# Merging the first input loads of a matmul kernel and giving one head cast to GpSimd

## The chip, the cores and the metric

One core of one Trainium2 chip. The metric is the device time of one execution in microseconds (us). TensorE is called PE in the profile, its weight load PEld, VectorE DVE, ScalarE ACT, GpSimd POOL, SyncE SP. All loads but the small one of the bias, and all stores, are issued by SP, and each of them is spread over 16 DMA engines. PSUM is the memory in which TensorE leaves its results; an eviction takes them out of it. A DMA has "landed" when the trace records its completion. The "head" is the part before the steady stream of tiles, some 18 us.

## The reference

```python
x = randn(16, 512, 1024); weight = randn(1024, 768)
bias = randn(768);        residual = randn(16, 512, 768)      # all float32
out = matmul(x, weight) + bias + residual
```

The kernel treats x as 8192 rows: 64 "tiles" of 128 rows, in 8 groups (S) of 8. Partition p of group S holds 8 consecutive rows; a load of "tiles 0 to 2" brings three rows of 1024 numbers to each of 128 partitions.

## The kernel before

Each tile is cast to bf16, transposed on TensorE (as four blocks of packed pairs), copied out of PSUM by VectorE, multiplied by the bf16 weights in 16 matmuls, evicted with bias or residual by VectorE, added to by GpSimd, and stored. In the head the first three tiles share the weights as they arrive. The parts that matter (cuts marked `...`):

```python
    load_x(0, 0, 2)
    load_x(0, 2, 3)
    load_w(0); load_w(1); load_w(2); load_w(3)
    load_x(0, 3, 4)
    load_x(0, 4, 6)
    load_x(0, 6, 8)
    load_res(0, 0, 4)
    load_x(1, 0, 4)
    ...
    keep_warm(12)                 # dummy matmuls, 128x512
    cast(0, "dve")
    cast(1)                       # ScalarE
    transp(0)                     # TensorE transposes into pt[t % 2], VectorE copies to xt
    transp(1)
    keep_warm(3)
    cast(2)
    transp(2)
    ...                           # bias broadcast by four matmuls, weight casts
    cast(HEAD, "dve")             # HEAD = 3: tile 3
    cast(HEAD + 1)
    for c in range(n_c):          # n_c = 4 blocks of the weights
        for t in range(HEAD):
            mms(t, 2 * c)
            mms(t, 2 * c + 1)
            if c == n_c - 1 and t == 0:
                finish(0)         # VectorE eviction
                pool_add(0)
            if c == n_c - 1 and t == 1:
                transp(HEAD)
    finish(1)
    ...
    for t in range(HEAD, n_t):    # steady state, one tile after another
        cast(t + 2)
        ...
```

## Time and profile before

| quantity | value | view |
|---|---|---|
| time | 210.83 us (210.65 to 210.95) | three runs |
| span of the profiled run | 209.0 us | page |
| TensorE busy | 200.4 us, 96% | page, part 1 |
| DMA queue q1 | 97.9% of 16 engines, 87.03 MB | page, part 3 |
| TensorE's last work ends | 203.06 us | chain of waits |
| last store issued, landed | 203.54 us, 205.19 to 208.13 us by engine | trace records |

From the page of the kernel before: busy times, then the DMA row of the 40 slices (tenths), the queue, and the chain by engine and by line.

```profile
PE 200.4 (96%) x1274; PEld 130.6 (63%) x1299; DVE 105.0 (50%) x139; ACT 67.6 (32%) x68; POOL 115.5 (55%) x71
...
DMA  6999999999999999999999999999999999999994
...
q1 hardware_dynamic: 5616, 87.03, 97.9%
...
PE 96%; issue 1%; DVE 1%
PE po L104 79%; PE pt L95 13%; PE po L170 3%; PE po L190 1%; DVE xt L99 0%; DVE ro L131 0%; DVE warm L156 0%
```

Two resources look full. To choose between them, follow the chain of waits in order of time (columns: start us, duration us, what). L170 are dummy matmuls, L95 transposes, L190 the bias matmuls, L104 the real matmuls.

```profile
1.19 5.26 PE po L170 x12
6.45 0.87 PE pt L95 x8
7.33 0.65 PE po L170 x3
7.97 0.44 PE pt L95 x4
8.41 1.29 PE po L190 x4
9.70 2.92 PE po L104 x18
...
199.15 3.91 PE po L104 x24
203.06 0.02 issue
203.08 0.42 DVE ro L131
```

It reads like a pure TensorE kernel, in which a late head would be paid at the end. But the chain stops at 203.50 us, the end of the last eviction, and the span is 209.0 us; the last 5.5 us, in which the last stores land, are in no share of the chain. The windows view covers them (first column: the stretch; last two: busy share of the 16 DMA engines, GB/s).

```profile
203.00:204.00 1.00, 0.05 (x1) 0.00 (x0) 0.42 (x1) 0.00 (x0) 0.00 (x0) 1.00 0.98 403
204.00:205.00 1.00, 0.00 (x0) 0.00 (x0) 0.00 (x0) 0.00 (x0) 0.00 (x0) 1.00 0.95 374
205.00:206.00 1.00, 0.00 (x0) 0.00 (x0) 0.00 (x0) 0.00 (x0) 0.00 (x0) 1.00 0.66 255
206.00:207.00 1.00, 0.00 (x0) 0.00 (x0) 0.00 (x0) 0.00 (x0) 0.00 (x0) 1.00 0.31 116
207.00:208.00 1.00, 0.00 (x0) 0.00 (x0) 0.00 (x0) 0.00 (x0) 0.00 (x0) 0.83 0.10 35
```

When TensorE ends, the DMA engines are still nearly full (0.98, then 0.95), and they then run dry one by one. The trace also records 16 landings for each of these DMAs, which I read as one from each engine. For the last store (128 KB, issued at 203.54) they are, in us, sorted:

```
205.19 205.22 205.25 205.38 205.52 205.56 206.38 206.43 206.56 206.65 206.69 206.83 206.84 207.32 208.06 208.13
```

The quickest engine lands its share 1.65 us after the issue. The slowest takes 4.59 us. My reading is that it still has older work in its queue; then the difference, 2.94 us, is roughly how much later the last store could be issued without moving the end.

The head of the kernel before, from the timeline (start us, duration us, engine, line, operation, count, [idle before, and what ended it]):

```profile
5.40 1.05 ACT L87 CAST xb<-x_tile 128x1024 bf16<-128x1024 f32 x1 [1.89 <-DMA x_tile<-in_x_dram]
5.40 0.69 DVE L87 CAST xb<-x_tile 128x1024 bf16<-128x1024 f32 x1 [4.13 <-DMA x_tile<-in_x_dram]
6.65 1.05 ACT L87 CAST xb<-x_tile 128x1024 bf16<-128x1024 f32 x1 [0.20 <-DMA x_tile<-in_x_dram]
...
15.47 0.70 DVE L87 CAST xb<-x_tile 128x1024 bf16<-128x1024 f32 x1 [0.71 <-DMA x_tile<-in_x_dram]
16.24 0.96 DVE L129 TENSOR_TENSOR tmp<-po,bias_sb 128x768 f32<-128x768 f32 x1
...
17.32 0.69 DVE L99 COPY xt<-pt 128x512 f32<-128x512 f32 x1
...
18.07 1.09 PEld L104 LDWEIGHTS <-xt 128*128 128x128 bf16 x8 [0.52 <-DVE xt L99]
```

The first two tiles are cast at 5.40 us, the third at 6.65 us, tile 3 at 15.47 us, and tile 3's matmuls, the start of the steady stream, begin at 18.07 us.

### The profile page before, as it was taken

The page shows a single profiled execution, that of the slowest core. Times are in us where ns is not written, and L with a number is a line of the kernel's source. Part 1 is how long each engine was busy: PE and PEld are TensorE (multiplying, and loading weights), DVE is VectorE, ACT ScalarE, POOL GpSimd, SP SyncE. Part 2 cuts the span into 40 slices and gives each one's busy share as a digit, 9 for nine tenths or more (in the row PEclk, how much of TensorE's full clock was granted, in tenths as well). Part 3 has the DMA queues.
Part 4 walks back from the last instruction along what each step waited for, and adds up shares of the span by engine and source line. Part 5 has one row for each costly group of instructions (what it writes and reads, how often), then busy time and mean ns, then how long its engine had stood idle before and what let it go on. Part 6 is the DMA issues. An engine that isn't in the chain of part 4 may idle for free.

```text
span 209.0 us, 3151 instructions
## 1 busy us (share of the span) xinstructions
PE 200.4 (96%) x1274; PEld 130.6 (63%) x1299; DVE 105.0 (50%) x139; ACT 67.6 (32%) x68; POOL 115.5 (55%) x71
## 2 busy tenths in 40 slices
PE   7999999999999999999999999999999999999980
PEld 2566666666666666666666666666666666666650
DVE  0737465445445544554554455455445544545550
ACT  2544315511723062422443054230724233430000
POOL 2000197819965565999189802994069910799000
PEclk9999999999999999999999999999999999999998
DMA  6999999999999999999999999999999999999994
GB/s 239 427 421 431 436 413 440 442 405 436 423 470 422 419 428 398 459 420 436 433 400 472 416 427 447 412 439 412 437 445 414 445 419 427 442 419 428 426 404 168
DMA packets 5632, 87.23 MB, mean 417 GB/s; under 512 B 625, under 2 KB 753, under 8 KB 1906
## 3 DMA queue, kind: packets, MB, share of 16 engines
q1 hardware_dynamic: 5616, 87.03, 97.9%
q8 instruction: 10, 0.16, 0.3%
q14 instruction: 4, 0.03, 0.0%
q10 hardware_dynamic: 2, 0.00, 0.0%
HBM read 61.87 MB, written 25.17 MB: 416 GB/s over the span
## 4 chain that ended last, share of the span: by engine, by line
PE 96%; issue 1%; DVE 1%
PE po L104 79%; PE pt L95 13%; PE po L170 3%; PE po L190 1%; DVE xt L99 0%; DVE ro L131 0%; DVE warm L156 0%
## 5 line engine op out<-in xcount | busy, mean ns | idle before, releaser
L104 PE MATMUL po<-w_sb,xt 128*128 128x512 bf16 (+1 forms) x999 | 175.4, 324 | 1.4
L104 PEld LDWEIGHTS <-xt 128*128 128x128 bf16 x1024 | 100.1, 98 | 59.5 <-DVE xt L99 0.5
L87 ACT CAST xb<-x_tile 128x1024 bf16<-128x1024 f32 x62 | 62.8, 1044 | 114.5 <-DMA x_tile<-in_x_dram 56.9
L121 POOL TENSOR_TENSOR ro<-ro,bias_sb 128x768 f32<-128x768 f32 x40 | 71.2, 1816 | 36.2 <-DMA ro<-in_residual_dram 26.2
L99 DVE COPY xt<-pt 128x512 f32<-128x512 f32 x64 | 44.2, 691 | 86.7 <-PE pt L95 86.5
L121 POOL TENSOR_TENSOR ro<-ro,tmp 128x768 f32<-128x768 f32 x24 | 43.1, 1814 | 41.0 <-DMA ro<-in_residual_dram 30.2
L131 DVE TENSOR_TENSOR ro<-po,ro 128x768 f32<-128x768 f32 (+2 forms) x41 | 38.0, 930 | 2.9 <-PE po L104 2.8
L95 PE MATMUL pt<-ident,xb 128*128 128x128 f32 x256 | 38.2, 273 | 0.0
L95 PEld LDWEIGHTS pt<-ident,xb 128*128 128x128 f32 x256 | 29.8, 141 | 8.1 <-issue 0.6
L129 DVE TENSOR_TENSOR tmp<-po,bias_sb 128x768 f32<-128x768 f32 x24 | 22.8, 949 | 0.6 <-POOL ro L121 0.5
L170 PE MATMUL po<-warm 128*128 128x512 bf16 x15 | 6.1, 579 | 1.2 <-DVE warm L156 1.2
L176 ACT CAST w_sb<-ro 128x768 bf16<-128x768 f32 x4 | 3.3, 832 | 4.0 <-DMA ro<-in_weight_dram 4.0
L170 PEld LDWEIGHTS <-warm 128*128 128x128 bf16 x15 | 1.9, 135 | 4.1 <-issue 2.8
L87 DVE CAST xb<-x_tile 128x1024 bf16<-128x1024 f32 x2 | 1.4, 696 | 4.8 <-DMA x_tile<-in_x_dram 4.8
L178 DVE CAST w_sb<-ro 128x768 bf16<-128x768 f32 x4 | 2.2, 555 | 2.5 <-DMA ro<-in_weight_dram 2.5
L161 ACT ACT_TABLE_LOAD x1 | 1.3, 1283 | 2.0 <-POOL ident masks.py:199 2.0
L190 PE MATMUL po<-tmp 128*128 128x512 f32 (+1 forms) x4 | 1.5, 486 | 0.0
L198 DVE COPY bias_sb<-po 128x768 f32<-128x768 f32 x1 | 1.0, 958 | 0.1
L190 PEld LDWEIGHTS po<-tmp 128*128 128x128 f32 x4 | 0.7, 190 | 0.5 <-issue 0.5
L135 POOL MEMSET tmp<- 128x768 f32 x1 | 0.7, 737 | 0.3 <-POOLq L268 0.3
L156 DVE MEMSET warm<- 128x256 uint32 x1 | 0.3, 272 | 0.9 <-PEq L268 0.9
masks.py:199 POOL TENSOR_SCALAR_AFFINE_SELECT ident<-ident 128x128 f32<-128x128 f32 x1 | 0.3, 292 | 0.1
(8 smaller groups left out, 1.0 us busy)
## 6 DMA issues: line engine op xcount, KB each, us to landing
ro<-in_residual_dram SPq DMA_DIRECT2D x7, 3072.0 KB, 18.1
out_dram<-ro SPq DMA_DIRECT2D x7, 3072.0 KB, 23.9
x_tile<-in_x_dram SPq DMA_DIRECT2D x5, 4096.0 KB, 30.8
x_tile<-in_x_dram SPq DMA_DIRECT2D x4, 2048.0 KB, 27.6
x_tile<-in_x_dram SPq DMA_DIRECT2D x3, 1024.0 KB, 8.6
ro<-in_weight_dram SPq DMA_DIRECT2D x4, 768.0 KB, 9.0
ro<-in_residual_dram SPq DMA_DIRECT2D x2, 1536.0 KB, 21.1
out_dram<-ro SPq DMA_DIRECT2D x1, 1536.0 KB, 11.9
```

Source lines behind the costliest of these rows:

```text
L87: K_(copy(out=xb[t], in_=x_sb[t // J][:, t % J, :]))
L95: K_(nc.tensor.transpose(out=pt[:, c, :], in_=pairs[:, c * P:(c + 1) * P], identity=ident))
L99: K_(nc.vector.tensor_copy(out=xt[t], in_=pt))
L104: K_(nc.tensor.matmul(po[t][:, n0:n0 + nl], lhsT=both[:, e, :], rhs=w_sb[:, c, e, n0:n0 + nl], start=(i == 0), stop=(i == len(steps) - 1),))
L121: K_(nc.gpsimd.tensor_add(out=r, in0=r, in1=tmp[t] if t < EARLY else bias_sb))
L129: K_(nc.vector.tensor_add(out=tmp[t], in0=p, in1=bias_sb))
L131: K_(nc.vector.tensor_add(out=row(t, n0, nl), in0=p, in1=row(t, n0, nl)))
L161: K_(nc.scalar.copy(out=warm_a, in_=warm_a))
L170: K_(nc.tensor.matmul(warm_ps[:, 0:512], lhsT=warm[:, 0:P], rhs=warm, start=True, stop=True))
L176: K_(nc.scalar.copy(out=w_sb[:, c, e, :], in_=w_st[:, c, e, :]))
L178: K_(nc.vector.tensor_copy(out=w_sb[:, c, e, :], in_=w_st[:, c, e, :]))
L190: K_(nc.tensor.matmul(bias_ps[:, n0:n0 + nl], lhsT=ones, rhs=bias_row[:, n0:n0 + nl], start=True, stop=True,))
```

## The change

Its intent: fewer, larger loads in the head. The first three tiles come in one DMA, the other five of the group in two (two tiles, three tiles). Since the first three now land together, the third cast goes to GpSimd so that three engines cast at once; two dummy matmuls move ahead of the first transposes to cover the later start.

```diff
-            copy = nc.scalar.copy if engine == "act" else nc.vector.tensor_copy
+            copy = {"act": nc.scalar.copy, "dve": nc.vector.tensor_copy,
+                    "pool": nc.gpsimd.tensor_copy}[engine]
...
-    load_x(0, 0, 2)
-    load_x(0, 2, 3)
+    load_x(0, 0, 3)
     load_w(0) ... load_w(3)
-    load_x(0, 3, 4)
-    load_x(0, 4, 6)
-    load_x(0, 6, 8)
+    load_x(0, 3, 5)
+    load_x(0, 5, 8)
...
-    keep_warm(12)
+    keep_warm(14)
     cast(0, "dve"); cast(1); transp(0); transp(1)
-    keep_warm(3)
-    cast(2)
+    keep_warm(1)
+    cast(2, "pool")
     transp(2)
```

More of the change, by code (lines that the diff above doesn't have):

```diff
@@ L85, in cast @@
             xb[t] = ring(sb, "xb", t, 4, [P, K], BF16)
-            copy = nc.scalar.copy if engine == "act" else nc.vector.tensor_copy
+            copy = {
+                "act": nc.scalar.copy, "dve": nc.vector.tensor_copy,
+                "pool": nc.gpsimd.tensor_copy,
+            }[engine]
             K_(copy(out=xb[t], in_=x_sb[t // J][:, t % J, :]))
```

## The prediction

> What bounds the kernel now. The page shows TensorE busy 96% and the DMA queue q1 97.9%. The chain of waits is almost pure TensorE: from 1.19 us to 203.06 us it never stops for more than 0.7 us, and every row tile costs 3.04 us, so the chain says that any delay in the head is a delay at the end. The tail contradicts it. The windows view shows all 16 DMA engines still full (shares 0.95 to 1.0) up to 205 us, after TensorE has ended. The trace records 16 landings for every DMA, one for each engine: the last store, 128 KB issued at 203.54, landed at 205.19 on the quickest engine and at 208.13 on the slowest. The slowest engine has a backlog since about 2 us; it sets the end. The lag comes in steps of some 1.1 to 1.2 us, which is what each of the ten 16 KB instruction packets takes in the records (about 1.0 to 1.1 us); the Trainium skill ("Runtime: NRT & Kernel Launch", Instruction fetch mechanics) says that instructions come by DMA in 16 KiB blocks, and these records agree. So the binding resource is DMA, and TensorE has roughly 2 to 2.9 us of slack at the end.
>
> What the change does.
> - DMA: same bytes, two DMAs fewer; per engine 24 packets instead of 40 for the first x block. Packets take 159 ns (4 KB), 314 (8 KB), 461 (12 KB): 10.08 against 9.89 us per engine, 0.19 us saved, an estimate from these medians.
> - First casts start when three tiles have landed, about 6.6 us (third tile before: 6.65) instead of 5.40. Transposes of tile 0 begin at about 7.4 instead of 6.3; two warm matmuls move ahead of them and fill it.
> - Third cast on GpSimd: its two-input adds of 768 take 1.82 us. The Trainium skill ("GPSIMD Engine Reference", Engine selection) calls one-input work roughly line rate, so I estimate 1.0 to 1.5 us for 1024. No run shows it yet. First real matmul at 10.2 to 11.3 instead of 9.7.
> - Weights land as before (8.5, 10.4, 12.3, 14.2).
> - Tile 3 now lands with tile 4, at about 16.7 instead of 15.45. On VectorE its cast (0.70), the first eviction (0.95) and the copy of the transposes (0.69) follow one another: tile 3's matmuls start at about 19.1 instead of 18.07. Either delay makes TensorE about 1.1 us (0.8 to 1.8) late, and its steady stream, with no slack, keeps this to the end: last matmul at about 204.2.
>
> Critical path: the TensorE delay fits into the DMA backlog; the last store is issued near 204.6 and waits in the slowest engine as before. Nothing starves earlier. What remains is 0.1 to 0.2 us saved in the queue.
>
> Predicted: 210.7 us, range 210.2 to 211.5. Chances: faster by over 2% 0.01, within 2% 0.97, slower by over 2% 0.02.
>
> What shows it right: tile 3's first matmul near 19.1 and last matmul 1 us or more later, while the last landing stays at 208 us; the spread of the last store's landings over the engines shrinks because the quick engines end later; GpSimd's cast at 1.0 to 1.5 us; DMA share 1.0 throughout.
>
> What would make it wrong: the last landing moving by the whole TensorE delay (TensorE bound after all: about 211.9); a GpSimd cast of several us, or a port lock, delaying the first matmul by over 3 us; a DMA queue that empties somewhere; instruction packets falling on the engines differently, which moves the slowest engine's lag by up to 1 us.

## The result, and the profile after

| | before | after |
|---|---|---|
| median of six runs | 210.85 us (210.58 to 211.35) | 210.94 us (210.81 to 211.00) |
| TensorE's last work ends | 203.06 us | 204.55 us |
| last store issued | 203.54 us | 205.03 us |
| its landing, quickest and slowest engine | 205.19, 208.13 us | 206.70, 208.08 us |

The ratio is 1.0003, with a 95% interval of 0.999 to 1.0016: the same time. A ratio here is the mean time of one kernel's fast runs over that of the other's of the same rounds, so it is not quite the ratio of the medians quoted. The experiments ran on other chips, so each is set against the kernel before on its own chip.

The chain of waits after, in order of time (the lines are L98 for transposes, L191 for the bias matmuls, L107 for the real matmuls):

```profile
0.74 6.16 DMA x_tile<-in_x_dram
6.90 0.02 issue
6.92 0.71 DVE xb L90
7.63 0.14 issue
7.76 0.64 PE pt L98 x4
8.41 0.02 issue
8.43 0.70 DVE xt L102
9.13 0.14 issue
9.27 0.63 PE pt L98 x4
9.89 1.29 PE po L191 x4
...
200.64 3.91 PE po L107 x24
204.55 0.02 issue
204.57 0.42 DVE ro L134
```

The head is visibly worse. The bias matmuls start at 9.89 us instead of 8.41, and the last block of matmuls at 200.64 instead of 199.15: 1.48 and 1.49 us. The first casts, which now wait for three tiles, begin at 6.92 us instead of 5.40 (1.52 us later), and nothing after them makes this up. All of the delay is made in the first ten microseconds and TensorE carries it, unchanged, through the whole kernel. Judged by the chain, this is a 1.5 us regression. The time does not show it, and the timeline and windows of the tail say why.

```profile
6.92 1.04 ACT L90 CAST xb<-x_tile 128x1024 bf16<-128x1024 f32 x1 [3.41 <-DMA x_tile<-in_x_dram]
6.92 0.69 DVE L90 CAST xb<-x_tile 128x1024 bf16<-128x1024 f32 x1 [5.65 <-DMA x_tile<-in_x_dram]
6.96 1.56 POOL L90 CAST xb<-x_tile 128x1024 bf16<-128x1024 f32 x1 [4.97 <-DMA x_tile<-in_x_dram]
...
16.90 0.70 DVE L90 CAST xb<-x_tile 128x1024 bf16<-128x1024 f32 x1 [1.92 <-DMA x_tile<-in_x_dram]
...
17.73 0.96 DVE L132 TENSOR_TENSOR tmp<-po,bias_sb 128x768 f32<-128x768 f32 x1
...
18.81 0.69 DVE L102 COPY xt<-pt 128x512 f32<-128x512 f32 x1
...
19.56 1.09 PEld L107 LDWEIGHTS <-xt 128*128 128x128 bf16 x8 [0.52 <-DVE xt L102]
```

```profile
203.00:204.00 1.00, 1.00 (x9) 0.65 (x7) 0.23 (x2) 0.00 (x0) 0.00 (x0) 1.00 0.69 289
204.00:205.00 1.00, 0.54 (x5) 0.23 (x3) 0.89 (x2) 0.00 (x0) 0.00 (x0) 1.00 0.93 378
205.00:206.00 1.00, 0.00 (x0) 0.00 (x0) 0.00 (x0) 0.00 (x0) 0.00 (x0) 1.00 0.83 321
206.00:207.00 1.00, 0.00 (x0) 0.00 (x0) 0.00 (x0) 0.00 (x0) 0.00 (x0) 1.00 0.54 190
207.00:208.00 1.00, 0.00 (x0) 0.00 (x0) 0.00 (x0) 0.00 (x0) 0.00 (x0) 0.70 0.09 34
```

From 203 to 204 us the DMA share is now 0.69 instead of 0.98: the quick engines wait for the late stores. From 206 to 207 us it is 0.54 instead of 0.31: they make up for it. In the last stretch, where only the slowest engines work, it is the same (0.09 against 0.10). The landings of the last store, issued at 205.03, agree:

```
206.70 206.73 206.75 206.75 206.76 206.77 206.78 206.80 206.81 206.86 206.87 206.88 206.91 207.55 208.02 208.08
```

Thirteen engines landed within 0.21 us of one another, 1.7 to 1.9 us after the issue: they had no backlog left. The slowest landed where it landed before. The spread went from 2.94 to 1.38 us.

### The profile page after: what moved, and what is told of

It is laid out like the page before. It is cut to its first block, busy times and chain, and to the rows that moved or that the text cites. A ratio compares the mean times of both kernels' runs of the same rounds, so it can differ in the third digit from the quotient of the medians.

```text
span 209.0 us, 3150 instructions
## 1 busy us (share of the span) xinstructions
PE 200.7 (96%) x1274; PEld 130.7 (62%) x1299; DVE 104.8 (50%) x139; ACT 67.2 (32%) x67; POOL 117.1 (56%) x72
## 4 chain that ended last, share of the span: by engine, by line
PE 93%; DMA 3%; DVE 1%; issue 1%
PE po L107 79%; PE pt L98 13%; DMA x_tile<-in_x_dram 3%; DVE xt L102 1%; PE po L191 1%; DVE xb L90 0%; DVE ro L134 0%
## 5 line engine op out<-in xcount | busy, mean ns | idle before, releaser
L107 PE MATMUL po<-w_sb,xt 128*128 128x512 bf16 (+1 forms) x999 | 175.4, 324 | 1.4
L107 PEld LDWEIGHTS <-xt 128*128 128x128 bf16 x1024 | 100.1, 98 | 59.5 <-DVE xt L102 0.5
L98 PE MATMUL pt<-ident,xb 128*128 128x128 f32 x256 | 38.3, 273 | 1.2 <-DVE xb L90 1.0
L98 PEld LDWEIGHTS pt<-ident,xb 128*128 128x128 f32 x256 | 29.9, 141 | 9.3 <-issue 2.1
L90 POOL CAST xb<-x_tile 128x1024 bf16<-128x1024 f32 x1 | 1.6, 1557 | 5.0 <-DMA x_tile<-in_x_dram 5.0
L191 PE MATMUL po<-tmp 128*128 128x512 f32 (+1 forms) x4 | 1.5, 486 | 0.0
L191 PEld LDWEIGHTS po<-tmp 128*128 128x128 f32 x4 | 0.7, 190 | 0.5 <-issue 0.5
```

Of the source, the lines that this page charges most:

```text
L90: K_(copy(out=xb[t], in_=x_sb[t // J][:, t % J, :]))
L98: K_(nc.tensor.transpose(out=pt[:, c, :], in_=pairs[:, c * P:(c + 1) * P], identity=ident))
L107: K_(nc.tensor.matmul(po[t][:, n0:n0 + nl], lhsT=both[:, e, :], rhs=w_sb[:, c, e, n0:n0 + nl], start=(i == 0), stop=(i == len(steps) - 1),))
L191: K_(nc.tensor.matmul(bias_ps[:, n0:n0 + nl], lhsT=ones, rhs=bias_row[:, n0:n0 + nl], start=True, stop=True,))
```

## The experiments

Theory A: the slowest DMA engine sets the end, and TensorE has up to 2.9 us of slack. Rival B: TensorE sets the end, as the chain says, and the merged loads paid its delay back. Two side questions are which part of the change makes the delay, and what the GpSimd cast costs. All kernels marked "light" belong to one idea: take enough bytes off the DMA engines that TensorE must set the end, and every delay in the head becomes visible in the time.

### Delay TensorE and nothing else: late_12

```diff
-    keep_warm(3)
+    keep_warm(15)
```

> The kernel before, with 12 more warm matmuls ahead of the third transposes: TensorE's steady stream starts about 2.6 us later (12 x 0.216 us). Theory A (the slowest DMA engine sets the end, TensorE has up to 2.9 us of slack there): the last store is issued near 206.1 us, its last landing stays at 208.1 us, time 210.8 (210.6 to 211.3). Rival B (TensorE sets the end, and the change's delay was paid back by cheaper loads): time 213.4.

Measured: 211.34 us (210.99 to 211.45) against 211.16 for the kernel before on that chip; ratio 1.0001 (0.9985 to 1.0017). TensorE's last work ended at 205.70 us, 2.64 us later than in the profile before; the last store was issued at 206.18 and landed between 207.84 and 208.81 us. A holds and B, which expected 2.6 us more, fails. Two details of A were missed: the time is just outside 210.6 to 211.3, and the last landing is 0.7 us later than the 208.1 expected. The kernel before was 0.3 us slower on this chip than on the other (211.16 against 210.83), which covers a part of that; by the ratio nothing was lost. The slack is nearly gone: 14 engines landed within 0.2 us.

### Delay it beyond the slack: late_24

```diff
-    keep_warm(3)
+    keep_warm(27)
```

> The same with 24 more, about 5.2 us. A: the slack is used up; the last store is issued near 208.7 us and lands 1.65 us later, at about 210.4 us; time 213.1 (2.2 us over before, not 5.2). B: 216.0.

Measured: 213.36 us (213.35 to 213.63), ratio 1.0103 (1.0088 to 1.0119), which is 2.2 us more than 211.16, as A said. TensorE ended at 208.64 us, 5.58 us late (not 5.2: in this trace the first load also landed 0.4 us later than in the one before, at 5.79 instead of 5.38). The last store was issued at 209.12 and landed between 210.80 and 211.02 us: no engine has a backlog left, and the end follows TensorE. A delay of 1.5 us cost nothing, 2.6 us nothing that can be told from noise, 5.6 us cost 2.2. That is slack of about 3 us, used up (5.6 less 2.2 gives 3.4; the landings gave 2.94).

### Relieve the DMA engines: light_before and light_after

The residual of the last four rows of each partition, in the last group, is not loaded; their eviction adds the bias instead, and GpSimd's four adds for them go too. The result lacks that residual; the comparison with the reference still passed within its tolerance.

```diff
+            if S == n_s - 1:
+                j1 = J // 2                       # in load_res
-        if 0 <= t < n_t:                          # in pool_add
+        if 0 <= t < n_t - J // 2:
-            ... in1=row(t, n0, nl)                # in finish
+            ... in1=row(t, n0, nl) if t < n_t - J // 2 else bias_sb[:, n0:n0 + nl]
```

> The kernel before, with the residual of the last four rows of each partition not loaded (1.57 MB of 87 MB; wrong result on purpose), TensorE's work unchanged. A: each DMA engine is relieved of about 3.6 us, more than the slack, so TensorE comes to set the end: last landing near 205.3 us, time 208.0 (2.8 us less). B: time unchanged, 210.8.

> The same relief in the kernel after. A: TensorE's 1.49 us of delay now shows: 1.4 us more than light_before, about 209.5. B: no difference from light_before.

Measured, on one chip: before 211.16, light_before 208.42 (208.17 to 208.54; ratio 0.9865), light_after 209.59 us (209.52 to 209.66; ratio 0.9922). Taking 1.6 MB off the DMA engines gained 2.7 us although TensorE's work did not change: B, which expected no gain, fails again. And with DMA relieved, the same change that had cost nothing costs 1.17 us (209.59 minus 208.42). TensorE ended at 203.40 and 204.56 us in the two, no earlier than without the relief (203.06 and 204.55), so the gain is not one of compute. The last store's 16 landings lie within 0.44 and 0.22 us: no engine is behind any more.

I expected 1.4 us, from the 1.49 us of delay. The missing part is in light_before, which lost time of its own at tile 8. From its timeline:

```profile
30.71 2.94 ACT L89 CAST xb<-x_tile 128x1024 bf16<-128x1024 f32 x3 [8.15 <-DMA x_tile<-in_x_dram]
31.81 0.42 PEld L97 LDWEIGHTS pt<-ident,xb 128*128 128x128 f32 x4 [0.43 <-ACT xb L89]
```

Tile 8's load arrives just in time for TensorE. In the profile before, its cast began at 30.34 us and the transposes did not wait; here it began at 30.71, their weight load waited 0.43 us, and they came 0.28 us later than before (31.81 against 31.53). In light_after TensorE comes later and does not wait there at all. A late head thus gives a little back at tile 8.

### Which part makes the delay: light_after_act, light_first_only, light_later_only

light_after_act is light_after with the third cast back on ScalarE:

```diff
-    cast(2, "pool")
+    cast(2)
```

> light_after with the third cast back on ScalarE. The trace of after ends the wait before the third transposes with VectorE's copy at 9.12 us, not with GpSimd's cast (done 8.52); on ScalarE the cast would end near 9.0. Theory A1: no change, 209.5 and first bias matmul within 0.1 us. Rival A2 (the GpSimd cast paces the head): a change of 0.4 us or more.

light_first_only is light_after with the later loads as before:

```diff
-    load_x(0, 3, 5)
-    load_x(0, 5, 8)
+    load_x(0, 3, 4)
+    load_x(0, 4, 6)
+    load_x(0, 6, 8)
```

> light_after with the later loads as before (one, two, two tiles): only the first load merged. A1: the first merge alone makes the 1.5 us, TensorE's head stays the pacer: same as light_after, about 209.5. Rival A3 (the late tile 3 makes the delay): 208.0 to 208.4.

light_later_only is light_before with only those later loads merged (the same edit, reversed).

> light_before with only the later loads merged (two, three). A1: tile 3's cast waits for 16.7 us, then cast, eviction and copy on VectorE follow one another, tile 3's matmuls start near 19.1 instead of 18.07: time 1.0 us over light_before, 209.0. Rival: the late tile is free, 208.0.

The three ran on another chip than light_before and light_after, one where the kernel before took 210.82 us. So compare the ratios and the ends of TensorE's work (one profile each), not the times across chips:

| kernel | TensorE ends | time | ratio to before |
|---|---|---|---|
| light_before | 203.40 us | 208.42 us | 0.9865 |
| light_later_only | 204.16 us | 209.04 us | 0.9911 |
| light_first_only | 204.45 us | 209.53 us | 0.9934 |
| light_after_act | 204.57 us | 209.53 us | 0.9933 |
| light_after | 204.56 us | 209.59 us | 0.9922 |

The GpSimd cast is worth nothing: with ScalarE doing it one after the other, TensorE ends 0.01 us away. The timeline of light_after_act shows what the third transposes do wait for:

```profile
6.94 1.99 ACT L92 CAST xb<-x_tile 128x1024 bf16<-128x1024 f32 x2 [3.42 <-DMA x_tile<-in_x_dram]
...
9.29 0.63 PE L100 MATMUL pt<-ident,xb 128*128 128x128 f32 x4 [0.22 <-DVE xt L104]
```

ScalarE's second cast is done at 8.93 us and the transposes still start at 9.29, when VectorE's copy of tile 0 has freed the PSUM buffer. There are two such buffers, and the third tile needs the first one again.

The first merge makes nearly all of the delay (204.45 against 204.56). light_first_only also keeps the GpSimd cast, which light_after_act clears, and the moved dummies; these are not in the chain of waits after, which runs from the load through the casts. The later merge alone also makes a delay (204.16, which is 0.76 us after light_before, less than the 1.0 expected), by the way the prediction described: VectorE casts tile 3 at 16.95 us, evicts tile 0 at 17.56, copies the transposes at 18.43, and tile 3's matmuls start at 19.17 us. In the full change that second delay is hidden behind the first: its cast of tile 3 begins at 16.90 us, but TensorE itself comes late to tile 3 (19.56 us). The two delays do not add, because they run in parallel up to the same point.

### Take TensorE's work away: half_matmuls

```diff
-            start=(i == 0), stop=(i == len(steps) - 1),
+            start=(i == 0), stop=(i == len(steps) // 2 - 1),   # and steps 4 to 7 return at once
```

> The kernel before, with only the first four of eight accumulation steps (wrong result on purpose): TensorE's work falls by some 85 us, all loads and stores stay. A: the end stays with the slowest DMA engine; about half of the ten instruction packets vanish with the instructions, which takes 1.0 to 1.6 us off its lag: 209.5 (209.0 to 210.5). Rival B: the time falls by what DMA leaves idle, 4 us or more.

Measured: 209.97 us (209.62 to 210.10), ratio 0.9953 (0.9938 to 0.9967); the result is wrong. From its page:

```profile
PE 134.9 (65%) x787; PEld 79.2 (38%) x787; DVE 105.0 (51%) x139; ACT 66.2 (32%) x68; POOL 115.1 (55%) x71
...
q1 hardware_dynamic: 5616, 87.03, 98.4%
q8 instruction: 6, 0.10, 0.2%
```

TensorE's busy time fell by 65.5 us, not by the 85 expected, and the time by 0.5%. The granted clock was lower here (mean 0.948), but that is not the reason: from 10 to 100 us it was 1.00 in both kernels, and there too busy time fell only by a third (from 89.2 to 61.0 us). The reason stays open. The last store was issued at 194.41 us, nine microseconds earlier than before, and landed between 204.97 and 207.00. The instruction packets fell from ten to six and the spread over engines from 2.94 to 2.03 us. This fits the idea that instruction packets, each on one engine, make the lag of the slowest one. The landings of earlier loads in the two traces support it. In the kernel before, the 16 landings of a load lie within 0.34 us until the first instruction packet starts at 21.5 us; those of the next load (23.78 to 25.34 us) spread over 1.56 us, the last of them 1.22 us behind the other fifteen. In half_matmuls the first packet comes later, at 32.7 us, and so does the step: the landings of loads up to 32.9 us still lie within 0.54 us, those of the next one (37.30 to 39.05 us) over 1.76 us. Which engine a packet went to is not recorded, and not every later packet adds a step, so the whole spread of 2.94 us is not accounted for.

### The GpSimd cast by itself: pool_alone

In the kernel after, tile 0's cast goes to ScalarE too, so that VectorE is idle while GpSimd casts.

```diff
-    cast(0, "dve")
+    cast(0)
```

> The kernel after, with the cast of tile 0 on ScalarE too, so that VectorE does nothing while GpSimd casts tile 2. In after that cast took 1.56 us beside VectorE's 0.69 us cast, which began 0.04 us earlier. P1 (VectorE's cast holds the shared port and GpSimd waits for its end): alone it takes 0.9 to 1.0 us. P2 (GpSimd's own rate for this conversion): 1.5 to 1.6 us again. Time: within noise of after in either case, 210.9 plus or minus 0.4.

```profile
6.91 1.04 POOL L90 CAST xb<-x_tile 128x1024 bf16<-128x1024 f32 x1 [4.92 <-DMA x_tile<-in_x_dram]
```

Alone it takes 1.04 us, beside VectorE's cast 1.56 us: P1 holds (a little over its 0.9 to 1.0) and P2 fails. The 0.52 us of difference are most of the 0.65 us for which VectorE's cast was still running (6.96 to 7.61). The Trainium skill ("SBUF — State Buffer", Who interferes with whom) says that VectorE, in an instruction of a two-port mode, and GpSimd contend for one pair of ports under an exclusive lock, that a cast can enter such a mode, and that the later one "fully blocks". No record names the mode of this cast; the two durations agree with the lock, and VectorE, which began 0.04 us earlier, kept its 0.69 us. The one timed run took 210.96 us (kernel before on that chip: 211.44, one run), which says nothing more about the time.

No experiment pointed to a correct version faster than both kernels. What helped was fewer bytes (2.7 us) or half of the matmuls (0.5%), both with a wrong result.

## Why the prediction was right

- The binding resource. Predicted: the slowest DMA engine, with 2 to 2.9 us of slack for TensorE. Shown by late_12, late_24, light_before and light_after; the slack is about 3 us.
- TensorE's delay. Predicted 1.1 us (0.8 to 1.8), measured 1.49. The mechanism was half right. The prediction left two delays open ("either") and named a sign of the late tile 3, matmuls near 19.1 through VectorE's queue; in the full change it is the first merge that sets the pace, and light_later_only shows that the other delay exists but is hidden. That 1.49 fell into the range is in part luck.
- The head. First load expected at 6.6 us, landed at 6.90. Third transposes were expected to wait for GpSimd; they waited for VectorE's copy that frees the PSUM buffer. First real matmul expected between 10.2 and 11.3 us, came at 11.19.
- GpSimd's cast. Estimated 1.0 to 1.5 us, measured 1.56: the rate was right (1.04 alone) and the rest came only beside VectorE's cast, as pool_alone shows.
- Weights "as before". They landed 0.21 to 0.24 us later (8.76, 10.63, 12.52, 14.39 against 8.52, 10.41, 12.29, 14.18).
- The saving of 0.19 us in the queue is the term that was not seen. The whole first group had landed at 20.42 us before and at 20.56 after. One trace each cannot settle 0.19 us: with the old loads (five traces) that landing lies between 20.42 and 20.83, with all three merged (four traces) between 20.45 and 20.60. The median is 0.09 us higher, not 0.1 to 0.2 lower, and all of it is within noise.
- Of the signs named, these were seen: last landing at 208.08 us (before 208.13), spread down to 1.38 us, tile 3's matmuls late (19.56, not 19.1, instead of 18.07). Two were not: GpSimd's cast was just over its range, and the DMA share did not stay at 1.0; it fell to 0.69 from 203 to 204 us.

## What to carry to other kernels

The chain of waits ends with the last instruction, not with the last landing, so a kernel that shows "96% TensorE" can still end with a DMA engine: compare the landings of the last store on the quickest and the slowest engine, and their difference is a first estimate of the slack that compute has (here 2.94 us, and about 3 by late_12 and late_24). Where such slack exists, a change in the head can be slower on its own path and cost nothing, and one that is faster there should gain nothing (not tested here); test it with the other resource relieved before you believe either. Merging loads also postpones the first use of the data to the landing of the last piece, which here cost 1.5 us of TensorE and saved nothing measurable in the queue.

## What the Trainium skill lacked or had wrong

- "Runtime: NRT & Kernel Launch", Instruction fetch mechanics, describes instruction fetch in 16 KiB blocks as hidden behind the issue of instructions. The packets are here (ten of 16 KB, 0.94 to 1.10 us each on the DMA engines), but in a DMA-limited kernel their DMA time need not be hidden: the slowest engine ended 2.94 us after the quickest with ten packets and 2.03 us after with six. The first packet is followed by a step of 1.2 us in the landings, at 21.5 us in one kernel and at 32.7 us in the other; that packets cause the whole spread was not isolated.
- "GPSIMD Engine Reference", Engine selection, says that one-input work is roughly line rate, with no figure for a cast: 128x1024 from float32 to bf16 took 1.04 us alone, as long as on ScalarE (1.05), and 1.56 us beside a VectorE cast (0.69).
- "SBUF — State Buffer", Who interferes with whom, has the later instruction fully blocked. GpSimd grew by 0.52 us where VectorE's cast still had 0.65 us to run, so some 0.13 us of its own time seem to pass during the wait, an estimate from these durations. This need not contradict the page.
- No page that I read says to compare the 16 landings of the last store with one another; here it is what told slack (2.94 us) from the bound.
